# Latent values evicted into the places of dead keys and masks; query latents, near latents and the first latent weight split elsewhere

## The chip, the cores and the metric

The program runs on one core of one Trainium2 chip. The core has a matrix engine (TensorE, PE in the tables), three engines for elementwise work (VectorE or DVE, ScalarE or ACT, GpSimd or POOL), and queues that start transfers (SP's above all). The metric is the time of one execution in microseconds, as the median of several runs; less is better.

## The reference

Two transformer layers run over 128 context tokens and 512 latent tokens with the same weights. The first layer mixes tokens by two kinds of heads, eight of each: multi-head latent attention (MLA), whose keys and values are expanded from a short latent vector per token, and neighbourhood attention on a grid of width 64. The second has grouped-query attention. Each is followed by a SwiGLU block. All is float32. The change lies at the seam of the two kinds of heads in the first layer:

```python
def mla_expand(ckv, w_ukv, k_rope):
    kv = (ckv @ w_ukv).reshape(b, L, MLA_HEADS, MLA_NOPE_DIM + MLA_V_DIM)
    k_nope, v = kv[..., :MLA_NOPE_DIM], kv[..., MLA_NOPE_DIM:]
    k_r = jnp.broadcast_to(k_rope[:, :, None, :], (b, L, MLA_HEADS, MLA_ROPE_DIM))
    return jnp.concatenate([k_nope, k_r], axis=-1), v

def even_mixer_latent(h, c_ckv, c_krope, c_nk, c_nv, w_in, q_norm, w_uq, kv_norm, w_ukv, rpb, w_out, cos, sin):
    q, ckv, krope, nq, nk, nv = even_project(h, w_in, q_norm, w_uq, kv_norm, w_ukv)   # q = rms_norm(cq) @ w_uq
    q = jnp.concatenate([q[..., :MLA_NOPE_DIM], apply_rope(q[..., MLA_NOPE_DIM:], cos, sin)], axis=-1)
    krope = apply_rope(krope[:, :, None, :], cos, sin)[:, :, 0, :]
    k_lat, v_lat = mla_expand(ckv, w_ukv, krope)
    k_ctx, v_ctx = mla_expand(c_ckv, w_ukv, c_krope)
    a_mla = attend_blocked(q, jnp.concatenate([k_lat, k_ctx], axis=1),
                           jnp.concatenate([v_lat, v_ctx], axis=1), MLA_SCALE)
    a_na = neighbourhood_attention(nq, nk, nv, c_nk, c_nv, rpb)
    return jnp.concatenate([a_mla.reshape(b, L, -1), a_na.reshape(b, L, -1)], axis=-1) @ w_out

def reference(...):
    for l in range(DEPTH):                       # two layers; context (xp) and latents (xs) alike
        hs = modulate(rms_norm(xs, norm_mix[l]), sh1_s, sc1_s)
        out_s = even_mixer_latent(hs, ...) if l % 2 == 0 else odd_mixer_latent(hs, ...)
        xs = xs + g1_s * out_s
        hs = modulate(rms_norm(xs, norm_ffn[l]), sh2_s, sc2_s)
        xs = xs + g2_s * swiglu(hs, w_ffn_in[l], w_ffn_out[l])
    y_sample = rms_norm(xs, norm_final)
```

## The kernel before

Tokens stand in the columns, 640 of them (512 latents, then 128 of context), features in the 128 partitions. Every operand of a matrix product is kept as two tiles of a rounded format: a high part, which ScalarE writes by a copy, and a low part, the rest, which VectorE writes by a subtraction. This is called a split here. A product is three matmuls: high by high, high by low, low by high (`mm3`). The names end in `h` and `l` for the two parts.

Work is written as small pieces, and a string sets their order: `NA_FIRST`, `NA_ORDER` and `NA_LAST` for the eight neighbourhood heads (`for h in range(8)`), `MLA_FIRST`, `MLA_ORDER` and `MLA_LAST` for the eight MLA heads. `sequence` runs the pieces of a string one after the other. TensorE follows the strings; on ScalarE and VectorE a scheduler orders what the pieces issue, and `after(inst, fn)` keeps an instruction behind another one of the same engine. Each engine works strictly in its own order.

A neighbourhood head h has these pieces. `s0` and `s1` make the scores of four blocks of queries (`ns`), VectorE adds the mask and bias `bm` and takes the maximum (`np`, `nm`), ScalarE takes the exponentials, GpSimd divides by the sums. In the string of the next head stand its tail pieces: `t0` to `t2` transpose the weights (`nt`) and split them (`nts`, in `pt_split`), `v0` to `v2` multiply them with the values (`no`), and the result is added up in `oN`. `sp`, `pt` and `pv` (`npp`) are the same for the context tokens. Two tiles `bm` are used in turn, keys `nk0` and `nk1` are made for two heads at a time, and `nkc` holds the cached keys.

In the last two heads, h = 6 and 7, the work for MLA is woven in, since no projections are left there:

- `latents()` splits the latent vectors `ckv`: the `far` ones (`ck`, the 512 latents) and the `near` ones (`ckp`, cached and context). It runs behind h = 5, in front of the strings of h = 6.
- `mla_w(0)` splits the first MLA weight, `wm`.
- `x0` in h = 6 splits the query latents (`cqs`). `k0` and `k1` make the keys of the first two MLA heads (`mk`) and split them into `kT` and `kTp`; `mk` uses `far` latents first, `near` ones in `k1`.
- `x` in h = 7 splits the rotary keys `kr` into their places in `kT` and `kTp`.
- `u0` and `u1` make the first MLA query (`mq`); `b0` to `b3` multiply four blocks of latents with the value weight `wmv` (`mv_product`, banks `mv`), `b4` and `b5` follow within the first MLA head.
- The products `b0` to `b3` stay in their banks until the neighbourhood pool `ab` is closed. Then the tiles `mv` are opened in the next pool, `cp`, and `vsplit` evicts them.

The first MLA scores (`ms`, `mla_scores`) use the same banks, opened anew by `open_y(s=2)`.

Of the kernel before, what the change touches and what calls it, by code (L numbers as in the profile page):

```python
# [50 lines left out]
def body(ctx, tc, xT, vecs, crow, wm0, wm0g, wm1, wA, wNV, wNA, wMK, wMV, wOA, wGQ, wGK, wGV, wOC,  # L51
# [326 lines left out]
    def pt_split(ps, n, pool, name):  # L378
        bufs = 5 if pool.name == "cp" else 3
        h = pool.tile([P, 512], F32R, tag="pth", bufs=bufs, name=name + "h")  # L380
        l = pool.tile([P, 512], F32R, tag="ptl", bufs=bufs, name=name + "l")
        S.activation(h[:, :n], ps[:, :n], AF.Copy)
        V.tensor_tensor(l[:, :n], ps[:, :n], f(h[:, :n]), ALU.subtract)
# [60 lines left out]
    def vsplit(dst, src):  # L444

        s3 = src.rearrange("p (h d) -> p h d", d=64)
        S.activation(dst[:, :, 0:64], s3, AF.Copy)
        V.tensor_tensor(dst[:, :, 64:128], s3, f(dst[:, :, 0:64]), ALU.subtract)
# [62 lines left out]
    with tc.tile_pool(name="start", bufs=1) as big:  # L511
# [143 lines left out]
    nc.sync.dma_start(ckf, cnkT)  # L655
    nkc = ab.tile([P, 8, P], F32R, name="nkc")
    for r in range(2):
# [53 lines left out]
    def na_k(p):  # L711
        get = wna(p, 1)
        ks = [ab.tile([P, 1024], F32R, tag=f"nk{r}", bufs=1, name=f"nk{p}{r}") for r in range(2)]
        nqk[p][2] = ks
        out = []
        for c, (c0, c1) in enumerate(((0, 256), (256, T))):
            def done(ps, c=c):
                if c == 1:
                    kf = ab.tile([P, P], F32, tag="nkf", bufs=1, name=f"nkf{p}")
                    S.activation(kf, ps[:, 256:384], AF.Copy)  # L720
                    nc.gpsimd.dma_start(o_nkT[p], kf)
                for r in range(2):
# [6 lines left out]
                    mark[0] = S.activation(h, src, AF.Copy), V.tensor_tensor(l, src, f(h), ALU.subtract)
                    if c == 0:  # L730
                        G.tensor_scalar(ks[r][:, 768:896], f(ks[r][:, 0:P]), 1.0, 0.0, ALU.mult, ALU.add)
                        for i in (2, 4):
                            G.tensor_scalar(ks[r][:, P * i:P * i + P], f(nkc[:, 2 * p + r, :]), 1.0, 0.0, ALU.mult, ALU.add)
            out += pieces_of(f"nk{p}{c}", qbanks[c], get, hh, hl, list(range(KT)), c0, c1, done)
        return out

    bms = [ab.tile([P, 3, 384], F32, name=f"bm{i}") for i in range(2)]
    for bm in bms:
# [83 lines left out]
    def latents():  # L822
        cc = load(cckvT.rearrange("u p n -> p u n"), 256, "cc")
        near = [ring.tile([P, T], F32R, tag="x", name=f"ckp{c}") for c in "hl"]
        far = [[ring.tile([P, T], F32R, tag="h" + c, name=f"ck{c}{u}") for u in range(2)] for c in "hl"]
        for u in range(2):
            after(mark[0][0], lambda: S.activation(far[0][u][:, :NS], ckv[u][:, :NS], AF.Copy))
            after(mark[0][1], lambda: V.tensor_tensor(far[1][u][:, :NS], ckv[u][:, :NS], f(far[0][u][:, :NS]), ALU.subtract))
        nh, nl = [t[:, :512].rearrange("p (u n) -> p u n", u=2) for t in near]
        src = cc.rearrange("p (u n) -> p u n", u=2)  # L830
        after(mark[0][0], lambda: S.activation(nh[:, :, 0:P], src, AF.Copy))
        after(mark[0][1], lambda: V.tensor_tensor(nl[:, :, 0:P], src, f(nh[:, :, 0:P]), ALU.subtract))
        for u in range(2):
            after(mark[0][0], lambda: S.activation(nh[:, u, P:], ckv[u][:, NS:T], AF.Copy))
            after(mark[0][1], lambda: V.tensor_tensor(nl[:, u, P:], ckv[u][:, NS:T], f(nh[:, u, P:]), ALU.subtract))
        return far, [[t[:, 256 * u:256 * u + 256] for u in range(2)] for t in near]

# [55 lines left out]
    def mv_product(i, bk):  # L893
        def run():
            mvb.append(bk(f"mv{i}"))
            for u in range(2):
                a, b = [t[u][:, i % 4 * P:(i % 4 + 1) * P] for t in lat[i // 4]]
                mm3(mvb[i], a, b, wmv[0][:, 512 * u:512 * (u + 1)], wmv[1][:, 512 * u:512 * (u + 1)], u == 0, u == 1)
            if mv:
                vsplit(mv[i], mvb[i])  # L900
        return run

    mv = []

    def mq_ring(h):
# [5 lines left out]
                "s0 q0 t0 t1 q1 m0 q2 s1 v0 t2 sp q3 q4 v1 q5 q6 q7 m1 v2 m2")  # L911
    NA_LAST = "s0 t0 t1 s1 x0 v0 t2 pt k0 sp v1 k1 v2 pv", "s0 t0 t1 u0 s1 u1 v0 t2 b0 sp x v1 b1 v2"
    for h in range(8):
# [52 lines left out]
    nc.sync.dma_start(tq, tabM)  # L966
# [1255 lines left out]
```

## Time and profile before

| | |
|---|---|
| median of 3 runs | 1495.97 us (1495.92 to 1497.59) |
| profiled execution | 1495.85 us, of which the span of its instructions 1494.1 |
| mean granted TensorE clock in it | 0.993 |
| TensorE busy | 1445.6 us, 97% of the span |
| VectorE busy | 1210.5 us, 81% |
| ScalarE busy | 762.8 us, 51% |
| GpSimd busy | 207.3 us, 14% |
| read and written in memory | 192.23 and 34.69 MB, 152 GB/s |

The profile shows one execution. "Idle before" and brackets name what ended an engine's waiting. A row of the timeline has its start and length in us, the engine, the line, the operation, what it writes and reads, and how many there are. The granted clock is the share of TensorE's full clock in a stretch. Busy time on TensorE counts slow work too, so the clock has to be read beside it.

### The profile page before, as it was taken

The numbers are of one execution on the slowest core, as the hardware profiler recorded it, in microseconds if no ns is written. First come the engines' busy times: TensorE is split into PE (matmuls) and PEld (weight loads), VectorE is DVE, ScalarE is ACT, GpSimd is POOL, SyncE is SP. The second block draws the span as 40 slices with busy tenths as digits, with TensorE's granted clock in tenths as the row PEclk, the third lists the DMA queues.
The fourth block names the chain that finished last, engine by engine and source line by source line (L and its number), as shares of the span: only waits on it lengthen the run. The fifth ranks groups of instructions, "written<-read, shape, count | busy, mean of one in ns | idle before, by whom it ended". The sixth has DMA issues, their size and how long they took to land.

```text
span 1494.1 us, 25710 instructions
## 1 busy us (share of the span) xinstructions
PE 1445.6 (97%) x9785; PEld 1395.6 (93%) x9785; DVE 1210.5 (81%) x2278; ACT 762.8 (51%) x1509; POOL 207.3 (14%) x298
## 2 busy tenths in 40 slices
PE   5999988999999999999999999999999999999996
PEld 4988878889999999999999999989999999999996
DVE  5786687986899999977998878775899999954496
ACT  5445677873755454441123666663755555542242
POOL 0325634432000000000001312222000000000000
PEclk9999999999999999999999999999999999999998
DMA  9544410105155555569764311003155555668522
GB/s 373 215 146 155 150 58 18 43 29 191 50 180 173 187 180 180 181 214 337 272 214 132 114 33 37 33 20 130 49 180 178 181 193 206 211 222 309 194 85 71
DMA packets 79900, 228.59 MB, mean 153 GB/s; under 512 B 8865, under 2 KB 14273, under 8 KB 79393
## 3 DMA queue, kind: packets, MB, share of 16 engines
q1 hardware_dynamic: 76544, 219.40, 42.9%
q0 software_dynamic: 1600, 5.14, 0.9%
q10 hardware_dynamic: 1632, 2.43, 0.5%
q8 instruction: 76, 1.25, 0.3%
q14 instruction: 48, 0.39, 0.1%
HBM read 192.23 MB, written 34.69 MB: 152 GB/s over the span
## 4 chain that ended last, share of the span: by engine, by line
PE 84%; DVE 7%; ACT 5%; issue 2%; DMA 1%; DVEq 0%; ACTq 0%; SPq 0%
PE fg L63 20%; PE fd L63 9%; PE fo L63 8%; PE fu L63 6%; PE gq L63 3%; PE nk L63 2%; PE fo_0b L63 1%; PE fo_2b L63 1%; PE gs L63 1%; PE nq L63 1%; PE fo_2a L63 1%; PE fo_0a L63 1%; PE go L63 1%; PE mod L63 1%; PE ms L63 1%
## 5 line engine op out<-in xcount | busy, mean ns | idle before, releaser
L1759 DVE SCALAR_TENSOR_TENSOR junk<-wm,cb 128x1024 bf16<-128x1024 f32 x62 | 75.7, 1220 | 5.7 <-DMA wm<-in_wm 5.1
L1211 ACT ACTIVATE sg<-g 128x320 f32<-128x320 f32 x34 | 16.0, 472 | 114.9 <-DVE g L1211 114.9
L63 PE MATMUL gq<-h10h,wgq 128*128 128x320 f32 x256 | 66.7, 318 | 0.0
L255 POOL TENSOR_SCALAR h10h<-h10t,gs,mods 128x320 fp32r<-128x320 f32 x4 | 3.6, 891 | 429.5 <-DVE h10t L249 427.8
L1211 DVE SCALAR_TENSOR_TENSOR junk<-wm,cb 128x1024 bf16<-128x1024 f32 x50 | 61.0, 1221 | 0.8
L1211 DVE TENSOR_TENSOR wY<-s,wY 128x1024 fp32r<-128x1024 f32 x40 | 48.8, 1219 | 1.2 <-ACT wY L1211 1.1
L1211 DVE TENSOR_TENSOR wZ<-s,wZ 128x1024 fp32r<-128x1024 f32 x40 | 48.8, 1219 | 0.0
L63 PEld LDWEIGHTS gq<-h10h,wgq 128*128 128x128 f32 x256 | 45.0, 188 | 0.9 <-PE gtp L67 0.2
L1211 ACT ACTIVATE wZ<-s 128x1024 fp32r<-128x1024 f32 x40 | 42.4, 1060 | 0.1
L1211 ACT ACTIVATE wY<-s 128x1024 fp32r<-128x1024 f32 x40 | 42.0, 1049 | 0.0
L1941 ACT ACTIVATE gp<-gs,gb,rq 128x640 f32<-128x640 f32 (+1 forms) x40 | 31.8, 796 | 16.1 <-DVE gb L1940 15.8
L63 PE MATMUL gq<-h10l,wgq 128*128 128x320 f32 x128 | 39.5, 308 | 0.0
L63 PE MATMUL fg<-h11E,wW 128*128 128x320 f32 x240 | 38.7, 310 | 0.0
L63 PE MATMUL fg<-h01q,wX 128*128 128x320 f32 x240 | 38.6, 309 | 0.0
L63 PE MATMUL fg<-h11q,wX 128*128 128x320 f32 x240 | 38.6, 309 | 0.0
L63 PE MATMUL fg<-h11N,wZ 128*128 128x320 f32 x240 | 38.6, 309 | 0.0
L63 PE MATMUL fg<-h01N,wZ 128*128 128x320 f32 x240 | 38.6, 309 | 0.0
L63 PE MATMUL fu<-h11q,wX 128*128 128x320 f32 x240 | 38.6, 309 | 0.0
L63 PE MATMUL fu<-h01q,wX 128*128 128x320 f32 x240 | 38.6, 309 | 0.0
L63 PE MATMUL fg<-h01E,wW 128*128 128x320 f32 x240 | 38.6, 309 | 0.0
L63 PE MATMUL fg<-h11C,wY 128*128 128x320 f32 x240 | 38.5, 309 | 0.0
L63 PE MATMUL fd<-h11q,wZ 128*128 128x320 f32 x240 | 38.5, 309 | 0.0
(3224 smaller groups left out, 5250.6 us busy)
## 6 DMA issues: line engine op xcount, KB each, us to landing
wm<-in_wm SPq DMA_DIRECT2D x48, 512.0 KB, 3.7
mraw<-in_wm SPq DMA_DIRECT2D x8, 1024.0 KB, 15.3
mraw<-in_wm SPq DMA_DIRECT2D x16, 512.0 KB, 3.7
hr_T<-sp_T SPq DMA_DIRECT2D x21, 320.0 KB, 5.8
hr_B<-sp_B SPq DMA_DIRECT2D x18, 320.0 KB, 6.4
mrow<-in_wm0g POOLq DMA_DIRECT2D x8, 512.0 KB, 6.4
wm<-in_wm0g SPq DMA_DIRECT2D x8, 512.0 KB, 3.5
x<-in_xT SPq DMA_DIRECT2D x8, 320.0 KB, 5.3
```

What stands on the lines that cost most here:

```text
L63: cls.last = nc.tensor.matmul(*a, **k)
L255: G.tensor_scalar(h[:, c0:c1], t, self.gsl[:, k, 0:1], self.ml[:, self.sh + k, 0:1], ALU.mult, ALU.add)
L1211: self.last = after(self.last, lambda: op(*a, **k))
L1759: def step(kind, at, line=lambda op, *a, **k: op(*a, **k)):
L1941: S.activation(dst, src, AF.Exp, bias=nb, scale=rq[:, j:j + 1], accum_out=ll[:, j:j + 1])
```

## The change

The four evictions that waited for the pool's end now follow their products at once. Five of the six value tiles lie in a new pool `aa`, which outlives `ab`, at the places of tiles that are no longer used by then: `nkc`, `nk0`, `bm0`, `nk1`, `bm1` (`tag` names the place). The near latents leave `latents()` for `latents_near`, called in `x0`; `x0` stands before `s1` instead of behind it, and the splits in it stand behind the last transposes' split (`cut`) instead of the last exponential or maximum (`mark`). The rotary keys (`x`) go from h = 7 to the end of h = 6. The first MLA weight is split between the two halves of the last keys. A second place with the same idea in the second layer (`wgq`, `valued`) is also written.

```diff
 def pt_split(ps, n, pool, name):
-        S.activation(h[:, :n], ps[:, :n], AF.Copy)
-        V.tensor_tensor(l[:, :n], ps[:, :n], f(h[:, :n]), ALU.subtract)
+        cut[0] = (S.activation(h[:, :n], ps[:, :n], AF.Copy),
+                  V.tensor_tensor(l[:, :n], ps[:, :n], f(h[:, :n]), ALU.subtract))
...
     sb = ExitStack()
+    sa = ExitStack()
+    aa = sa.enter_context(tc.tile_pool(name="aa", bufs=1, reuse_waits="tile"))
     ab = sb.enter_context(tc.tile_pool(name="ab", bufs=1, reuse_waits="tile"))
-    nkc = ab.tile([P, 8, P], F32R, name="nkc")
+    nkc = aa.tile([P, 8, P], F32R, tag="nkc", name="nkc")
...
 def na_k(p):
-        ks = [ab.tile([P, 1024], F32R, tag=f"nk{r}", bufs=1, name=f"nk{p}{r}") for r in range(2)]
+        ks = [aa.tile([P, 1024], F32R, tag=f"nk{r}", bufs=1, name=f"nk{p}{r}") for r in range(2)]
...
                     mark[0] = S.activation(h, src, AF.Copy), V.tensor_tensor(l, src, f(h), ALU.subtract)
+                    if c == 0 and p == 3 and r == 1:
+                        mla_w(0, mark[0])
...
-    bms = [ab.tile([P, 3, 384], F32, name=f"bm{i}") for i in range(2)]
+    bms = [f(aa.tile([P, 3, 384], F32R, tag=f"bm{i}", name=f"bm{i}")) for i in range(2)]
...
 def latents():
+        return far, [[t[:, 256 * u:256 * u + 256] for u in range(2)] for t in near], near, cc
+
+    def latents_near(near, cc):
         nh, nl = [t[:, :512].rearrange("p (u n) -> p u n", u=2) for t in near]
-        after(mark[0][0], lambda: S.activation(nh[:, :, 0:P], src, AF.Copy))
+        after(cut[0][0], lambda: S.activation(nh[:, :, 0:P], src, AF.Copy))
...
 def mv_product(i, bk):
-            if mv:
-                vsplit(mv[i], mvb[i])
+            if i < 5:
+                mv[i] = aa.tile(([P, 9, P] if i in (2, 4) else [P, 8, P]), F32R, tag=("nkc", "nk0", "bm0", "nk1", "bm1")[i], name=f"mv{i}")
+            vsplit(mv[i], mvb[i])
...
-    NA_LAST = "s0 t0 t1 s1 x0 v0 t2 pt k0 sp v1 k1 v2 pv", "s0 t0 t1 u0 s1 u1 v0 t2 b0 sp x v1 b1 v2"
+    NA_LAST = "s0 t0 t1 x0 s1 v0 t2 pt k0 sp v1 k1 v2 x pv", "s0 t0 t1 u0 s1 u1 v0 t2 b0 sp v1 b1 v2"
...
-                    for t, q in zip(rsplit(cq[u], f"cqs{u}", mark[0]), qlat):
+                    for t, q in zip(rsplit(cq[u], f"cqs{u}", cut[0]), qlat):
                         q.append(t)
+                latents_near(*rest_lat)
...
         if h == 5:
-            lat = latents()
-            mla_w(0, mark[0])
+            *lat, near, cc = latents()
+            rest_lat = near, cc
...
-    mv += [cp.tile([P, 8, P], F32R, name=f"mv{i}") for i in range(6)]
-    for i in range(4):
-        vsplit(mv[i], mvb[i])
+    mv[5] = cp.tile([P, 8, P], F32R, name="mv5")
...
-        get = lazy(lambda: unit(wGQ[h], 1024, f"wgq{h}"))
+        get = lazy(lambda: unit(wGQ[h], 1024, f"wgq{h}", behind=valued[0] if h == 1 else None))
...
     for i in (0, 1, 2, 3, 5, 4):
-        S.activation(gvh[i], srcs[i], AF.Copy)
-        V.tensor_tensor(gvl[i], srcs[i], f(gvh[i]), ALU.subtract)
+        valued[:] = [(S.activation(gvh[i], srcs[i], AF.Copy), V.tensor_tensor(gvl[i], srcs[i], f(gvh[i]), ALU.subtract))]
```

TensorE's rows stand in the same order before and after. What moves stands on ScalarE and VectorE. On VectorE, ahead of the first maximum of h = 7 (the row `np_0` with `bm`), before, with the sums `oN` of the last tail and the value weight's split:

```order
L852 TENSOR_TENSOR kTp<-mk_2559,kTp 64x128 x2
L394 TENSOR_TENSOR oN_1990<-no_2513,nhs_2578 64x448
L394 TENSOR_TENSOR oN_1990<-no_2513,nhs_2578 64x64
L185 TENSOR_TENSOR wmv<-wmvr,wmv 128x1024
L440 TENSOR_TENSOR oN_1990<-npp2o,npp2h 64x128 x2
L771 ISA np_0_2606,nm_2591<-ns_00_2600,bm_1010 128x384
```

and the same place now:

```order
L861 TENSOR_TENSOR kTp<-mk_2562,kTp 64x128
L396 TENSOR_TENSOR oN_1993<-no_2516,nhs_2581 64x448
L396 TENSOR_TENSOR oN_1993<-no_2516,nhs_2581 64x64
L861 TENSOR_TENSOR kTl_2425<-kr,kTh_2423 64x512
L861 TENSOR_TENSOR kTl_2426<-kr,kTh_2424 64x512
L861 TENSOR_TENSOR kTl_2425<-kr,kTh_2423 64x128
L861 TENSOR_TENSOR kTl_2426<-kr,kTh_2424 64x128
L861 TENSOR_TENSOR kTp<-kr,kTp 64x128 x2
L442 TENSOR_TENSOR oN_1993<-npp2o,npp2h 64x128 x2
L185 TENSOR_TENSOR wmv<-wmvr,wmv 128x1024
L778 ISA np_0_2621,nm_2606<-ns_00_2615,bm_1013 128x384
```

The six rows that read the rotary keys `kr` have moved ahead of that maximum. On VectorE ahead of the second pair of maxima of h = 6, where the query latents `cqs` and the near latents `ckp` stand, before:

```order
L415 TENSOR_REDUCE npp3m_2546<-npp3s_2543 128x1
L375 RECIPROCAL nr_3r<-nl_2434 128x1
L454 TENSOR_TENSOR cqs0l<-cqr_587,cqs0h 128x640
L454 TENSOR_TENSOR cqs1l<-cqr_592,cqs1h 128x640
L832 TENSOR_TENSOR ckpl<-cc,ckph 128x2x128
L835 TENSOR_TENSOR ckpl<-ckvr_735,ckph 128x128
L835 TENSOR_TENSOR ckpl<-ckvr_740,ckph 128x128
```

and now:

```order
L375 RECIPROCAL nr_0r<-nl_2431 128x1
L457 TENSOR_TENSOR cqs0l<-cqr_590,cqs0h 128x640
L375 RECIPROCAL nr_1r<-nl_2431 128x1
L457 TENSOR_TENSOR cqs1l<-cqr_595,cqs1h 128x640
L842 TENSOR_TENSOR ckpl<-cc,ckph 128x2x128
L845 TENSOR_TENSOR ckpl<-ckvr_738,ckph 128x128
L845 TENSOR_TENSOR ckpl<-ckvr_743,ckph 128x128
L778 ISA np_2_2500,nm_2430<-ns_10_2494,bm_1012 128x384
```

The five split rows stood behind that pair of maxima (and behind the last sum's reciprocal, `nr_3r`) and now stand ahead of it. On VectorE ahead of the first maximum of MLA (`mn`), where the value products `mv` are evicted, before:

```order
L383 TENSOR_TENSOR npp3ptl<-npp3t,npp3pth 128x256
L394 TENSOR_TENSOR oN_2431<-no_2789,nhs_2809 64x448
L394 TENSOR_TENSOR oN_2431<-no_2789,nhs_2809 64x64
L440 TENSOR_TENSOR oN_2431<-npp3o,npp3h 64x128 x2
L448 TENSOR_TENSOR mv_2836<-mv_2698,mv_2836 128x8x64
L448 TENSOR_TENSOR mv_2837<-mv_2733,mv_2837 128x8x64
L448 TENSOR_TENSOR mv_2838<-mv_2775,mv_2838 128x8x64
L448 TENSOR_TENSOR mv_2839<-mv_2792,mv_2839 128x8x64
L448 TENSOR_TENSOR mv_2840<-mv_2858,mv_2840 128x8x64
L984 TENSOR_REDUCE mn_0_2874<-ms_0_2867 128x1
```

and now:

```order
L451 TENSOR_TENSOR mv_2791<-mv_2784,mv_2791 128x8x64
L383 TENSOR_TENSOR npp3ptl<-npp3t,npp3pth 128x256
L451 TENSOR_TENSOR mv_2811<-mv_2804,mv_2811 128x8x64
L396 TENSOR_TENSOR oN_2428<-no_2801,nhs_2824 64x448
L396 TENSOR_TENSOR oN_2428<-no_2801,nhs_2824 64x64
L442 TENSOR_TENSOR oN_2428<-npp3o,npp3h 64x128 x2
L451 TENSOR_TENSOR mv_2867<-mv_2860,mv_2867 128x8x64
L993 TENSOR_REDUCE mn_0_2877<-ms_0_2870 128x1
```

The fourth product's eviction (`mv_2811`) has gone ahead of the last tail's sums; only the fifth is left behind them.

More of the change, by code (lines that the diff above doesn't have):

```diff
@@ L381, in pt_split @@
         l = pool.tile([P, 512], F32R, tag="ptl", bufs=bufs, name=name + "l")
-        S.activation(h[:, :n], ps[:, :n], AF.Copy)
-        V.tensor_tensor(l[:, :n], ps[:, :n], f(h[:, :n]), ALU.subtract)
+        cut[0] = (S.activation(h[:, :n], ps[:, :n], AF.Copy),
+                  V.tensor_tensor(l[:, :n], ps[:, :n], f(h[:, :n]), ALU.subtract))
         return h, l
+    cut = [None]
     def tr(out, in_):
@@ L446, in vsplit @@
         s3 = src.rearrange("p (h d) -> p h d", d=64)
+        dst = dst[:, 0:8, :]
         S.activation(dst[:, :, 0:64], s3, AF.Copy)
@@ L828, in latents @@
             after(mark[0][1], lambda: V.tensor_tensor(far[1][u][:, :NS], ckv[u][:, :NS], f(far[0][u][:, :NS]), ALU.subtract))
+        return far, [[t[:, 256 * u:256 * u + 256] for u in range(2)] for t in near], near, cc
+    def latents_near(near, cc):
         nh, nl = [t[:, :512].rearrange("p (u n) -> p u n", u=2) for t in near]
         src = cc.rearrange("p (u n) -> p u n", u=2)
-        after(mark[0][0], lambda: S.activation(nh[:, :, 0:P], src, AF.Copy))
-        after(mark[0][1], lambda: V.tensor_tensor(nl[:, :, 0:P], src, f(nh[:, :, 0:P]), ALU.subtract))
+        after(cut[0][0], lambda: S.activation(nh[:, :, 0:P], src, AF.Copy))
+        after(cut[0][1], lambda: V.tensor_tensor(nl[:, :, 0:P], src, f(nh[:, :, 0:P]), ALU.subtract))
         for u in range(2):
-            after(mark[0][0], lambda: S.activation(nh[:, u, P:], ckv[u][:, NS:T], AF.Copy))
-            after(mark[0][1], lambda: V.tensor_tensor(nl[:, u, P:], ckv[u][:, NS:T], f(nh[:, u, P:]), ALU.subtract))
-        return far, [[t[:, 256 * u:256 * u + 256] for u in range(2)] for t in near]
+            after(cut[0][0], lambda: S.activation(nh[:, u, P:], ckv[u][:, NS:T], AF.Copy))
+            after(cut[0][1], lambda: V.tensor_tensor(nl[:, u, P:], ckv[u][:, NS:T], f(nh[:, u, P:]), ALU.subtract))
     KPART = ((0, 512), (512, 640), (640, 768))
@@ L898, in run @@
                 mm3(mvb[i], a, b, wmv[0][:, 512 * u:512 * (u + 1)], wmv[1][:, 512 * u:512 * (u + 1)], u == 0, u == 1)
-            if mv:
-                vsplit(mv[i], mvb[i])
+            if i < 5:
+                mv[i] = aa.tile(([P, 9, P] if i in (2, 4) else [P, 8, P]), F32R, tag=("nkc", "nk0", "bm0", "nk1", "bm1")[i], name=f"mv{i}")
+            vsplit(mv[i], mvb[i])
         return run
-    mv = []
+    mv = {}
     def mq_ring(h):
@@ L936, in query_latents @@
                 for u in range(2):
-                    for t, q in zip(rsplit(cq[u], f"cqs{u}", mark[0]), qlat):
+                    for t, q in zip(rsplit(cq[u], f"cqs{u}", cut[0]), qlat):
                         q.append(t)
+                latents_near(*rest_lat)
             pieces["x0"] = query_latents
+            pieces["x"] = lambda: k_set((slice(64, 128), slice(0, 64)), (0, 1, 2), [kr[:, a:b] for a, b in KPART])
             pieces.update(named("k", k_pieces(0, ybank)))
@@ L942, in body @@
             wmv = unit(wMV, 1024, "wmv", behind=mark[0])
-            pieces["x"] = lambda: k_set((slice(64, 128), slice(0, 64)), (0, 1, 2), [kr[:, a:b] for a, b in KPART])
             pieces.update(named("u", mq_ring(0)))
@@ L1078, in body @@
     sb.close()
+    sa.close()
     l0.close()
@@ L1879, in keys @@
                 kps[v, c] = kns[v][:, c0:c1]
-    gqs, rope0 = {}, []
+    gqs, rope0, valued = {}, [], []
     def gqa_q(h):
-        get = lazy(lambda: unit(wGQ[h], 1024, f"wgq{h}"))
+        get = lazy(lambda: unit(wGQ[h], 1024, f"wgq{h}", behind=valued[0] if h == 1 else None))
         qh = gp.tile([P, T], F32R, tag="gqh", bufs=2, name=f"gqh{h}")
```

## The prediction

> **What bounds the kernel now.** I read the page first: busy shares and the chain that ended last.
>
> ```profile
> span 1494.1 us, 25710 instructions
> PE 1445.6 (97%) x9785; PEld 1395.6 (93%) x9785; DVE 1210.5 (81%) x2278; ACT 762.8 (51%) x1509; POOL 207.3 (14%) x298
> PE 84%; DVE 7%; ACT 5%; issue 2%; DMA 1%; DVEq 0%; ACTq 0%; SPq 0%
> ```
>
> TensorE (PE) carries 84% of the chain; time is won where PE waits or runs slowly. The edits that move rows all sit between the sixth head of the neighbourhood attention and the first MLA head, about 187 to 240 us (heads are counted from 1 here; h in the code is one less). PE's waits from 180 to 260 us, longest in total first:
>
> ```profile
> PE ms L63 <- DVE mv L448: 3.4, 1, 3.4
> PE mk L63 <- DVE ckpl L835: 2.8, 1, 2.8
> PE no L63 <- ACT nts_0h L382: 1.6, 1, 1.6
> PE no L63 <- DVE nts_0l L383: 1.0, 1, 1.0
> PE npp3t L67 <- DVE oN L394: 0.8, 1, 0.8
> ```
>
> Next I cut that place into windows of 3.4 us (columns: stretch, length, PE busy and count, granted clock, DMA):
>
> ```profile
> 198.80:202.20 3.40, 1.61 (x12) 1.00 0.01 2
> 202.20:205.60 3.40, 2.38 (x11) 0.50 0.36 116
> 205.60:209.00 3.40, 3.40 (x16) 0.50 0.01 2
> 226.10:229.50 3.40, 0.53 (x3) 1.00 0.59 193
> 229.50:232.90 3.40, 2.91 (x9) 0.50 0.00 0
> ```
>
> After a window with PE busy 1.61 or 0.53 of 3.40 us the granted clock is 0.50. It came back after windows with 3.40 and 2.91 busy, not after 2.38. So each long wait is paid twice: at half clock, work takes about double (eight transposes below: 207.44 to 209.00, against 192.03 to 192.82). The first drop costs half of 2.38 + 3.40, 2.9 us; the second half of 2.91, 1.5 us. PE in order of time (start, length, row, wait in brackets):
>
> ```profile
> 192.03 1.03 PE L67 MATMUL nt<-ident,np 128*128 128x128 f32 x8
> 192.82 0.42 PE L63 MATMUL ns<-nk,nqh 128*128 128x384 f32 x1
> 203.22 0.58 PE L63 MATMUL mk<-ckpl,wm 128*128 128x256 f32 x1 [2.81 <-DVE ckpl L835]
> 207.44 1.82 PE L67 MATMUL nt<-ident,np 128*128 128x128 f32 x8
> 209.00 0.41 PE L63 MATMUL mq<-cqs0h,wm 128*128 128x320 f32 x1
> 210.80 0.44 PE L63 MATMUL ns<-nk,nqh 128*128 128x384 f32 x1 [0.31 <-DVE nm L771]
> 221.02 0.41 PE L67 MATMUL npp3t<-ident,npp3p 128*128 128x128 f32 x2 [0.84 <-DVE oN L394]
> 225.03 0.68 PE L63 MATMUL mv<-wmv,ckph 128*128 128x512 f32 x2
> 229.99 0.87 PE L63 MATMUL ms<-kTh,mqh 128*128 128x320 f32 x2 [3.36 <-DVE mv L448]
> ```
>
> And VectorE (DVE), the engine that PE waits for here, with one GpSimd row of the same time:
>
> ```profile
> 195.12 0.94 DVE L185 TENSOR_TENSOR wm<-wm0r,wm 128x768 fp32r<-128x768 f32 x1
> 195.99 0.20 DVE L774 TENSOR_SCALAR nn<-nm 128x1 f32<-128x1 f32 x2
> 197.63 0.16 DVE L375 RECIPROCAL nr_1r<-nl 128x1 f32<-128x1 f32 x1 [0.18 <-ACT np L775]
> 200.38 0.17 DVE L375 RECIPROCAL nr_3r<-nl 128x1 f32<-128x1 f32 x1 [0.31 <-ACT np L775]
> 200.94 0.95 DVE L454 TENSOR_TENSOR cqs0l<-cqr,cqs0h 128x640 fp32r<-128x640 f32 x1 [0.39 <-ACT cqs0h L453]
> 203.29 1.38 DVE L852 TENSOR_TENSOR kTl<-mk,kTh 64x512 fp32r<-64x512 f32 x2
> 205.84 0.59 DVE L852 TENSOR_TENSOR kTl<-mk,kTh 64x128 fp32r<-64x128 f32 x2 [0.98 <-ACT kTp L849]
> 209.57 0.58 DVE L440 TENSOR_TENSOR oN<-npp2o,npp2h 64x128 f32<-64x128 f32 x2 [0.49 <-ACT npp2h L438]
> 210.18 0.56 DVE L771 CUSTOM_DVE_ANT_0 np<-ns,bm 128x384 f32<-128x384 f32 x1
> 215.80 0.69 DVE L852 TENSOR_TENSOR kTl<-kr,kTh 64x512 fp32r<-64x512 f32 x1
> 216.61 2.13 DVE L852 TENSOR_TENSOR kTl<-kr,kTh 64x512 fp32r<-64x512 f32 x3
> 216.92 1.29 POOL L881 TENSOR_TENSOR mql<-mqt,mqh 128x320 fp32r<-128x320 f32 x1
> 218.75 0.59 DVE L852 TENSOR_TENSOR kTp<-kr,kTp 64x128 fp32r<-64x128 f32 x2
> 227.36 3.08 DVE L448 TENSOR_TENSOR mv<-mv,mv 128x512 fp32r<-128x512 f32 x5
> ```
>
> From 193 to 210 us DVE is idle only for the bracketed 2.35 us. It bounds that stretch, and it is where the change adds work.
>
> **The change part by part.** The order of the matmuls is the same in both programs, so only waits and the clock can move.
>
> *Latent values evicted at once.* Before, the first MLA score at 229.99 stands behind five evictions in one group (227.36, 3.08 us), because its two banks held the third and fourth product. Now those two are evicted as soon as they are made, ahead of the last tail rows. PE finishes the fourth product some 1.4 us before 225.03 (tail rows of head 8 stand between) and needs its bank after the fifth product, which takes 229.99 - 3.36 - 225.03 = 1.6 us; a ScalarE (ACT) eviction and a DVE one take about 0.6 each in that group, so there are about 1.5 us in hand. The wait goes: 3.36 us, and with it the half clock, 1.5 us. What is late next is the table tq for the second head, needed some 4 us after that score; a transfer queued (225.22 below) behind the same row as before, so it keeps its distance to the work. The evictions fall where DVE has room only if it isn't behind; see the third rival.
>
> *Near and query latents, and the rotary keys.* The split of the near latents moves behind the first transposes of head 7 and the query latents into the same place, both ahead of the second pair of score maxima. The 2.81 wait of mk mostly goes; what is late next is its bank, which waits for the maxima that stand behind five split rows. DVE gets to them from 195.1 (the weight split there is gone) by 1.5 for small rows and the transposes' splits, about 2.4 for the five (0.95 for the first, shorter ones after) and 1.0 for two maxima: 200.0. I take mk at 199.8. But the rotary key splits (six DVE rows on kr) move from the end of head 8 to the end of head 7, ahead of the first maximum of head 8 (row 210.18), which PE needs for its next score bank, the row at 210.80. That is the added wait. Behind it on PE is everything of head 8.
>
> When does DVE get there? 210.18, less the weight split (195.12 to 195.99, 0.87), plus the rotary rows, less the idle time that can be filled. The rotary rows took 0.69 + 2.13 + 0.59 = 3.4 in the trace; the same shapes from mk took 1.38 + 0.59 and, with the last pair, 0.59 more, 2.56 in all. I take 2.56, since the slow group ran beside a long GpSimd row (216.92), and that row comes later in head 8 than the new place, and keep 3.4 as the bound. Of the 2.35 idle I let 1.85 be filled and 0.5 stay. So 210.18 - 0.87 + 2.56 - 1.85 = 210.0: PE passes its score bank 0.2 us earlier than before (bounds: 1.0 earlier when rows pack tighter, 0.9 later with 3.4).
>
> When does PE get there? From 203.22 to 210.80 it took 7.58 us, of which 0.31 waiting and 2.9 lost to the half clock, so 4.4 at full clock. From 199.8, with about 1.3 of small waits on the same DVE, that is 205.5, and PE then stands still for about 5 us. All that the removed waits (mk, and the 1.6 + 1.0 on nts) bring is used up there.
>
> A stop of 5 us covers more than half of some window, so the clock drops. Where the window edges fall isn't to be chosen: with the first edge 1.8 us or more into the stop the clock drops there and is back two windows later; at 1.0 to 1.8 it drops one edge later; under 1.0 the third window holds too little work to bring it back, as 2.38 did above. PE then works 2.7 to 6 us at half clock and loses half of it: 1.3 to 3.0, I take 2.2. The Trainium skill (TensorE: Matmul & The Clock Gate, Part 1: The HAM clock gate) says that the window is free-running, 3413 ns; the drops at 202.2 and 229.5, eight windows apart, agree.
>
> The wait of 0.84 at 221.02 goes too: DVE rows ahead of it (rotary keys) have left, and PE comes 2 us later.
>
> *Weight split at head 6.* Transfers of the near latents, the first weight and the table tq on SP's queue, and the DVE row behind the last keys:
>
> ```profile
> 168.45 0.38 SPq L164 DMA_DIRECT2D cc<-in_cckvT  x1
> 175.47 0.34 SPq L164 DMA_DIRECT2D wm0r<-in_wMK  x1
> 225.22 0.33 SPq L966 DMA_DIRECT2D tq<-in_tabM  x1
> 190.97 0.55 DVE L729 TENSOR_TENSOR nk<-nk,nk 64x384 fp32r<-64x384 f32 x1 [2.47 <-ACT nk L729]
> ```
>
> The first MLA weight's split (0.94) goes into those 2.47 us, in which DVE waits for ACT and ACT for PE's last keys: nothing on the path, and if the row slipped past 190.97 it would cost its 0.9 there. The weight's and the near latents' transfers change places on SP's queue, with a bias table between them. Issued at 168 and 175 and used past 188, both have over 10 us in hand, which hides the change of order; were that gone, PE would wait for a landing. *Places.* Evictions now wait for the last readers of keys and masks, which are done by then; cost 0. *GpSimd* does one low query half one row later; no wait of PE above names it: 0. *The edge on the second grouped-query weight* moves no row: 0.
>
> **Sum**, against the profiled execution (1495.85, span 1494.1 and 1.75 around it, 0.12 under the median): 0.2 + 0.84 - 2.2 + 3.36 + 1.5 = 3.7 us gained. From there to the end PE runs almost without waits, so it stays: 1492.3 at the level of the median.
>
> **Rivals.** (1) The clock doesn't drop at the new wait, or the wait is short since DVE rows pack tighter: 2.2 more, up to 1.0 more, about 1489.7. Against it: a wait of 2.81 sufficed before. The same page (HAM oscillation) holds idle gaps up to about 3.4 us harmless; by that a wait 1.6 us shorter than mine would keep the clock, but the trace's 2.81 with the drop at 202.2 disagrees.
>
> (2) DVE is later: 3.4 for the rotary rows (0.9 more) and the dear clock case (0.8 more) leave 2.0: 1494.0. For it: the only rows on kr that the trace has are the slow ones.
>
> (3) The change doesn't do what it says: the fourth value product isn't evicted in time, because DVE, late through head 8, comes to it more than 1.5 us later than I think, and 229.99's wait stays. Then 0.2 + 0.84 - 2.2 is all: 1497.1.
>
> (4) Slower: the clock stays at half through all of head 8, whose many short transposes keep windows thin. From 210.6 to the score there are 229.99 - 3.36 - 0.84 - 210.80 = 15.0 us of work; doubled, 15 lost instead of 2.2: 1505.1. It turns into a loss from 5.9 us lost, 11.8 us at half clock, the fourth window. Against it: the same kind of rows brought it back at 209.0 after one full window.
>
> **Chances.** Forecast (gain 2.5 to 5) 0.50, (1) 0.13, (2) 0.24, (3) 0.08, (4) 0.05. What a measurement tells from no change is 0.2%, 3.0 us, so faster means under 1493.0: nine tenths of the forecast and (1), 0.59. Same: the rest of the forecast, (2) and most of (3), 0.33. Slower 0.08. The range runs from (1) with everything in its favour, 1489.2, to short of (3), 1495.9; the forecast's own is 1491 to 1493.5.
>
> **What would show it.** Right: no wait of ms on mv, PE waiting 4 to 6 us for nm at head 8's second bank, the granted clock 0.50 right behind that, and no 0.50 at the first MLA score. Wrong if that wait is under 2 us or over 7, or if a new wait over 1 us stands in the first MLA head.

## The result, and the profile after

The changed kernel takes 1493.07 us in the median (1491.25 to 1495.14), the kernel before 1496.90 (1495.01 to 1497.84) in the same comparison; the ratio is 0.9977, 95% interval 0.9969 to 0.9985. That is 3.4 us faster (2.2 to 4.6). The prediction was 1492.3 within 1489.2 to 1495.9, and faster. Its profiled execution took 1493.43. Of its 13 runs the four with a mean granted clock of 0.990 or 0.991, the profiled one among them, took 1493.4 to 1495.1 us, the other nine 1491.3 to 1493.7. First the page of the changed kernel: span, busy time of the engines, chain that ended last.

```profile
span 1491.6 us, 25707 instructions
PE 1445.5 (97%) x9785; PEld 1395.5 (94%) x9785; DVE 1210.0 (81%) x2278; ACT 763.3 (51%) x1509; POOL 207.8 (14%) x298
PE 85%; DVE 7%; ACT 4%; DMA 2%; issue 2%; DVEq 0%; SPq 0%; ACTq 0%
```

The busy times are those of before within 0.5 us, so what moved is waiting and the clock. TensorE's longest waits from 180 to 260 us:

```profile
PE ns L63 <- DVE nm L778: 4.7, 1, 4.7
PE ns L63 <- DVE kTl L861: 1.6, 1, 1.6
PE no L63 <- DVE nn L781: 1.5, 1, 1.5
```

The waits of `ms` on `mv`, `mk` on `ckpl` and `npp3t` on `oN` are gone; the first row is the new wait at head 8's second score bank (the buffer that TensorE writes scores to; it is free again when the maxima have read it), at 213.35 in the list in order of time:

```profile
192.53 0.44 PE L63 MATMUL ns<-nk,nqh 128*128 128x384 f32 x1 [0.50 <-DVE nk L734]
196.86 0.50 PE L63 MATMUL no<-nts_0l,nv 128*128 128x512 f32 x1 [1.50 <-DVE nn L781]
201.73 0.28 PE L63 MATMUL mk<-ckph,wm 128*128 128x256 f32 x1
205.48 0.42 PE L63 MATMUL ns<-nk,nqh 128*128 128x384 f32 x1 [1.61 <-DVE kTl L861]
213.35 0.69 PE L63 MATMUL ns<-nk,nqh 128*128 128x384 f32 x1 [4.65 <-DVE nm L778]
224.77 0.38 PE L67 MATMUL npp3t<-ident,npp3p 128*128 128x128 f32 x2
229.82 0.45 PE L63 MATMUL ms<-kTh,mqh 128*128 128x320 f32 x2
232.95 0.31 PE L63 MATMUL mq<-cqs0h,wm 128*128 128x320 f32 x1
```

The granted clock (the column behind PE's busy time and count), in windows laid on the edges of its drops:

```profile
194.55:197.96 3.41, 1.75 (x10) 1.00 0.00 0
197.96:201.37 3.41, 3.41 (x13) 0.50 0.17 46
208.20:211.61 3.41, 0.50 (x4) 1.00 0.01 2
211.61:215.03 3.42, 1.68 (x6) 0.50 0.31 89
215.03:218.44 3.41, 3.41 (x13) 0.50 0.20 38
225.27:228.68 3.41, 3.41 (x24) 1.00 0.00 0
228.68:232.09 3.41, 3.41 (x19) 1.00 0.58 192
```

Half clock for two windows right behind the new wait, none at the first MLA score, as forecast; and one that was not forecast, at 197.96, behind a wait of only 1.50.

Executions differ by when the windows begin, so two spans compare badly. I compare one stretch, from the score row that waits 0.50 for `nk` (192.53) to the first `mq` row behind the first MLA score (232.95): 40.42 us. In the kernel before it runs between these rows, 42.98 us:

```profile
191.57 0.44 PE L63 MATMUL ns<-nk,nqh 128*128 128x384 f32 x1 [0.50 <-DVE nk L729]
...
234.55 0.31 PE L63 MATMUL mq<-cqs0h,wm 128*128 128x320 f32 x1
```

So this pair of executions shows 2.56 us gained in the stretch. From there to the end the waits are the same in both within 0.3 us. The lengths of that rest are not: over all the kernels below it took 1258.4 to 1261.8 us, so gains in the runs and in the stretch can differ by some us.

### The profile page after: what moved, and what is told of

It reads as the page before. It is cut to its first block, busy times and chain, and to the rows that moved or that the text cites. A ratio compares the mean times of both kernels' runs of the same rounds, so it can differ in the third digit from the quotient of the medians.

```text
span 1491.6 us, 25707 instructions
## 1 busy us (share of the span) xinstructions
PE 1445.5 (97%) x9785; PEld 1395.5 (94%) x9785; DVE 1210.0 (81%) x2278; ACT 763.3 (51%) x1509; POOL 207.8 (14%) x298
## 4 chain that ended last, share of the span: by engine, by line
PE 85%; DVE 7%; ACT 4%; DMA 2%; issue 2%; DVEq 0%; SPq 0%; ACTq 0%
PE fg L63 21%; PE fd L63 9%; PE fo L63 8%; PE fu L63 6%; PE gq L63 3%; PE nk L63 2%; PE nq L63 1%; PE fo_2b L63 1%; PE fo_0b L63 1%; PE gs L63 1%; PE fo_2a L63 1%; PE fo_0a L63 1%; PE go L63 1%; PE mod L63 1%; DMA mraw<-in_wm 1%
## 5 line engine op out<-in xcount | busy, mean ns | idle before, releaser
L63 PE MATMUL fg<-h11E,wW 128*128 128x320 f32 x240 | 38.7, 310 | 0.0
L63 PE MATMUL fg<-h01C,wY 128*128 128x320 f32 x240 | 38.5, 309 | 0.0
```

Source lines behind the costliest of these rows:

```text
L63: cls.last = nc.tensor.matmul(*a, **k)
```

## Experiments

Each was timed in five rounds against the kernel before (the whole change in the 13 runs above). They ran on two chips, so kernels are compared by their ratio to the kernel before on the same chip. "Gain" is one minus the ratio, times the median of before in that comparison, with its 95% interval; "stretch" is the length defined above in the one profiled execution, and in brackets what it is shorter than before's 42.98.

| kernel | ratio (interval) | gain, us | stretch, us |
|---|---|---|---|
| whole change | 0.9977 (0.9969 to 0.9985) | 3.4 (2.2 to 4.6) | 40.42 (2.56) |
| eviction alone | 0.9955 (0.9943 to 0.9968) | 6.7 (4.8 to 8.5) | 37.67 (5.31) |
| all but eviction | 1.0009 (1.0000 to 1.0018) | -1.3 (-2.7 to 0.0) | 44.07 (-1.09) |
| rotary keys back | 0.9966 (0.9953 to 0.9978) | 5.1 (3.3 to 7.0) | 37.15 (5.83) |
| latents back | 0.9969 (0.9959 to 0.9979) | 4.6 (3.1 to 6.1) | 37.98 (5.00) |
| rotary lows on GpSimd | 0.9953 (0.9940 to 0.9965) | 7.0 (5.2 to 9.0) | 37.76 (5.22) |
| eviction, query lows on GpSimd | 0.9986 (0.9977 to 0.9995) | 2.1 (0.7 to 3.4) | 41.32 (1.66) |
| rotary back, far and query lows on GpSimd | 0.9939 (0.9925 to 0.9952) | 9.1 (7.2 to 11.2) | 35.20 (7.78) |
| eviction, weight split early | 0.9969 (0.9956 to 0.9981) | 4.6 (2.8 to 6.6) | 36.73 (6.25) |
| exponentials first | 0.9979 (0.9970 to 0.9988) | 3.1 (1.8 to 4.5) | 38.44 (4.54) |
| the fastest, copies late | 0.9963 (0.9951 to 0.9976) | 5.5 (3.6 to 7.3) | 37.82 (5.16) |
| the same, one query low on DVE | 0.9966 (0.9954 to 0.9977) | 5.1 (3.4 to 6.9) | 38.19 (4.79) |
| weight split back | 0.9987 (0.9978 to 0.9996) | 1.9 (0.6 to 3.3) | 41.24 (1.74) |

My theory (1): the gain is the wait at the first MLA score with its half clock, and the rest of the change gives part of it back at head 8's second score bank. Rival (2): the gain comes from the earlier latents at `mk`. The edge on the weight in the second layer stays in all these kernels and is not tested by itself; in the traces the split of `wgq1` stands 38.7 us behind that of `wgq0` before and after, and the wait of `gs` on `gvl` is 2.2 in both.

**The eviction alone.** The kernel before, with this part of the change (and that edge):

```diff
+            if i < 5:
+                mv[i] = aa.tile(..., tag=("nkc", "nk0", "bm0", "nk1", "bm1")[i], name=f"mv{i}")
+            vsplit(mv[i], mvb[i])
```

> The kernel before with one part of the change: the value products are evicted as soon as they are made, into the places of dead keys and masks. Latents, rotary keys and first weight split stand as before. Theory 1 (the gain is the wait at the first MLA score and the half clock behind it; the rest of the change earns nothing): the wait of 3.36 goes and the 1.5 lost at half clock with it, the mk wait of about 2.8 stays, no new wait for nm over 1 us: 4.9 us under the kernel before, 4.0 to 5.5. That would be faster than the whole change. Theory 2 (the gain comes from the earlier latents at mk): within 1 us of the kernel before.

Its waits from 186 to 240 us and the first MLA score:

```profile
PE mk L63 <- DVE ckpl L840: 1.8, 1, 1.8
PE no L63 <- ACT nts_0h L382: 1.6, 1, 1.6
PE no L63 <- DVE nts_0l L383: 1.0, 1, 1.0
PE ns L63 <- DVE nm L776: 0.7, 1, 0.7
...
226.88 0.45 PE L63 MATMUL ms<-kTh,mqh 128*128 128x320 f32 x2
```

No wait and no half clock at the score, the waits of `no` on `nts` as before, and a gain of 6.7: twice that of the whole change, and the intervals do not overlap. The forecast of 4.9 lies within the interval. Theory 2 falls.

**All but the eviction.**

```diff
-            vsplit(mv[i], mvb[i])
+            if mv:
+                vsplit(mv[i], mvb[i])
...
+    mv += [cp.tile([P, 8, P], F32R, name=f"mv{i}") for i in range(6)]
+    for i in range(4):
+        vsplit(mv[i], mvb[i])
```

> The whole change but for the eviction: the third and fourth value product wait in their banks for the end of the neighbourhood heads, as before. Theory 1: no gain, since what mk and the transposes no longer wait is stood out again at the second score bank of head 8, with a half clock behind it: 0 to 1.5 us slower than the kernel before, the wait of the first MLA score on mv back at 2.5 to 3.5. Theory 2: 3 to 4 us faster than the kernel before, as the whole change is.

```profile
PE ns L63 <- DVE nm L778: 3.7, 1, 3.7
PE ms L63 <- DVE mv L451: 3.4, 1, 3.4
```

Both waits stand side by side, and there is no gain. Against the whole change (1.0009 less 0.9977) the eviction is worth 4.8 us there (3.0 to 6.6 from the two intervals); the forecast's 3.36 + 1.5 lies in it. The two profiled executions differ by 3.65 in the stretch; in this one no half clock stands behind the wait of 3.36.

**Rotary keys back in head 8.**

```diff
-    NA_LAST = "... k0 sp v1 k1 v2 x pv", "... b0 sp v1 b1 v2"
+    NA_LAST = "... k0 sp v1 k1 v2 pv", "... b0 sp x v1 b1 v2"
```

> The whole change, but the rotary keys are split in head 8 again, behind its first score rows, as before. Theory 1 (the six DVE rows on kr, 2.57 us, and the three ACT copies in front of the exponentials, 0.95, make most of the wait of 4.65 for nm at the second score bank of head 8): that wait falls to 1 to 2 us, the first maximum of head 8 comes 2.5 to 3.5 us earlier, and the whole is 2 to 3.5 us faster than with the whole change, about 1490.3. Theory 3 (the wait comes from rows stretched beside GpSimd and from late exponentials): it stays over 3.5 us, time within 0.5 us of the whole change. Theory 4 (the rows only move the wait to the end of head 8): the wait for nm falls, but a wait of 1 us or more stands at the first MLA score, time within 1 us of the whole change.

PE's row at the bank, and VectorE's first maximum of head 8:

```profile
210.03 0.69 PE L63 MATMUL ns<-nk,nqh 128*128 128x384 f32 x1 [0.57 <-DVE nm L778]
...
209.41 0.56 DVE L778 CUSTOM_DVE_ANT_0 np<-ns,bm 128x384 f32<-128x384 f32 x1
```

From the stretch's start the maximum comes after 209.41 - 192.76 = 16.65 us, against 212.74 - 192.53 = 20.21 with the whole change: 3.6 earlier, and the wait shrinks from 4.65 to 0.57 (PE, at half clock from 206.2, comes 0.5 later). The new strings moved less than expected. On ACT three copies of `kr` stand as early in the stretch as with the whole change, two of them (201.32, 0.95) right ahead of the exponential at 202.29, and VectorE still waits for that:

```profile
203.10 0.16 DVE L375 RECIPROCAL nr_2r<-nl 128x1 f32<-128x1 f32 x1 [1.06 <-ACT np L782]
```

So it is the early place of the rotary rows on VectorE that made the wait (theory 3 falls), and no wait on `kTl` or `mv` stands at the first MLA score (theory 4 falls). The times do not show it by themselves: the intervals of this kernel and the whole change overlap.

**Latents back.** Query and near latents at their old places (`x0` behind `s1`, the near ones in `latents()`).

```diff
-    NA_LAST = "s0 t0 t1 x0 s1 v0 t2 ...
+    NA_LAST = "s0 t0 t1 s1 x0 v0 t2 ...
-                latents_near(*rest_lat)
```

> The whole change, but query and near latents are split at their old places, behind the second score maxima of head 7; rotary keys stay early. Theory 1 (what is saved at mk is swallowed by the later wait on the same DVE): the mk wait is back at 2 to 3 us with a half clock, the wait for nm at head 8 is shorter by as much, time within 0.8 us of the whole change. Theory 2 (the earlier latents earn the gain): 2 to 3.5 us slower than the whole change.

```profile
202.18 0.39 PE L63 MATMUL mk<-ckpl,wm 128*128 128x256 f32 x1 [2.58 <-DVE ckpl L842]
...
210.74 0.44 PE L63 MATMUL ns<-nk,nqh 128*128 128x384 f32 x1 [3.97 <-DVE nm L778]
```

The `mk` wait is back at 2.58, and it is no slower than the whole change (intervals overlap): theory 2 falls again. Theory 1 had the sizes wrong, too: the wait for `nm` is shorter by 0.7 and not by 2 to 3, and the half clock of `mk` did not come in this execution.

**Which half of the rotary keys.** Their low parts on GpSimd, ACT's copies left where they were:

```diff
-            V.tensor_tensor(l, src, h, ALU.subtract)
+            eng.tensor_tensor(l, src, h, ALU.subtract)      # eng is G for kr, V otherwise
```

> The whole change, with the six low parts of the rotary keys computed on GpSimd instead of DVE, at the same place in the program; ACT's copies of them stay. It tells the two halves of theory 1 apart. DVE half (the six rows, 2.57 us, stand ahead of the first maximum of head 8): the wait of 4.65 for nm falls to 1.5 to 2.5 us, time 1.5 to 3 us under the whole change, about 1490.5. ACT half (the copies make the exponentials late, and DVE only waits for these): the wait stays over 3.5 us, time within 0.7 us of the whole change. Either way GpSimd has to be done before the first MLA score; a wait of ms for kTl would show that it isn't.

```profile
208.61 0.69 PE L63 MATMUL ns<-nk,nqh 128*128 128x384 f32 x1 [2.15 <-DVE nm L778]
```

The wait falls by 2.50, and the gain is twice the whole change's, with intervals that do not overlap. From the stretch's start the maximum comes after 17.07 us, 3.14 earlier: 2.57 is what the six rows took on VectorE, and the rest goes with `mk`, which ran at full clock here (the reciprocal `nr_2r`, which waited 1.14 with the whole change, comes 0.66 earlier). PE came 0.6 earlier, too. No wait on `kTl` stands at the first MLA score. Together with the rotary keys back in head 8, this shows the rows on VectorE as the cause of most of the wait. The other half, ACT's order, I tried by itself:

```diff
-            pieces["x"] = lambda: k_set(...)
+            pieces["x"] = lambda: after(mark[0][0], lambda: k_set(...))
```

> The whole change, but ACT's copies of the rotary keys are issued behind the last exponential of head 7 (in the whole change three of them, 1.6 us, stand ahead of its last two exponentials). DVE keeps the six rotary rows ahead of the first maximum of head 8. If late exponentials make DVE idle 1.14 us there: that idle piece falls under 0.5, the wait for nm falls from 4.65 to 3.5 to 4.2, time 0.5 to 1.5 us under the whole change. If the six rows alone make the wait: it stays at 4.3 or more, time within 0.5 us of the whole change.

The idle piece of 1.14 is gone, and the first maximum of head 8 comes 18.83 us into the stretch instead of 20.21. But the wait is 4.65 as before and the time the same as the whole change's (0.9979 against 0.9977): PE came earlier by as much, its clock not having dropped at `mk` in that execution. The late exponentials are real in the trace; that they cost time is not shown.

**Weight split back**, behind `latents()` as before the change:

```diff
-                    if c == 0 and p == 3 and r == 1:
-                        mla_w(0, mark[0])
...
+            mla_w(0, mark[0])          # behind latents(), at h == 5
```

> The whole change, but the first latent weight is split where it was, behind the second pair of maxima of head 7's start. The prediction's step (the row moves into idle time and takes 0.87 us out of the path of DVE to the first maximum of head 8): with it back the wait for nm grows by 0.5 to 0.9 and the time by 0.5 to 1.5 us over the whole change. Rival (the row is worth nothing, since DVE waits there for exponentials and for GpSimd): wait and time within 0.4 us and 0.6 us.

The stretch grows by 0.82 and the gain falls by 1.5 (intervals overlap). That fits the forecast of 0.87 for this step, but does not show it: the first maximum comes 1.35 later in the stretch, but PE comes 2.5 later (half clock behind drops at 197.2 and 207.4), and so the wait went down, to 3.54, instead of up. The reverse, the early split added to the eviction alone, isn't clear:

```diff
+                    if c == 0 and p == 3 and r == 1:
+                        mla_w(0, mark[0])
...
-            mla_w(0, mark[0])
```

> The eviction part alone (1489.5) with the first latent weight split behind the last neighbourhood keys, as the whole change has it. Prediction's reading (the row goes into idle time of DVE and ACT, and 0.9 us of DVE leave the stretch ahead of the transposes' split): the waits on nts and mk shrink by 0.5 to 1.5 in all, time 0 to 1.5 us under the eviction part alone. Rival (a row beside GpSimd's key copies is stretched and holds the keys up): up to 1 us over it, with a longer wait for nk.

The two waits on `nts` shrink, from 1.59 and 0.99 to 0.87 and 0.80, but that of `mk` grows from 1.75 to 2.59, so in all nothing is saved there. The stretch is 0.94 shorter than with the eviction alone, the gain 2 us less, with intervals that overlap. What the early split is worth stays open.

**GpSimd in place of VectorE.** Four tries at something faster. The eviction alone, with the low parts of the query latents on GpSimd:

```diff
-        after(at[1], lambda: V.tensor_tensor(l, src, f(h), ALU.subtract))
+        after(at[1], lambda: eng.tensor_tensor(l, src, f(h), ALU.subtract))      # G for cqs
```

> The eviction part alone (1489.5), with the two low parts of the query latents (1.6 us of DVE ahead of the near latents at mk) on GpSimd. If DVE's row order is what holds mk: its wait of 1.8 falls under 0.5, the half clock at 205 goes or comes once fewer, 1 to 2.5 us under the eviction part alone, about 1487.7. Rival: DVE rows beside GpSimd rows take as much longer as was saved, time within 0.6 us of the eviction part alone.

The wait of `mk` did not fall, it doubled, and 4.6 of the 6.7 are lost. PE, VectorE and GpSimd there:

```profile
206.74 0.58 PE L63 MATMUL mk<-ckpl,wm 128*128 128x256 f32 x1 [3.69 <-DVE ckpl L840]
...
204.74 1.74 DVE L837 TENSOR_TENSOR ckpl<-cc,ckph 128x256 fp32r<-128x256 f32 x1 [2.21 <-POOL cqs0l L457]
...
203.17 1.53 POOL L457 TENSOR_TENSOR cqs0l<-cqr,cqs0h 128x640 fp32r<-128x640 f32 x1
204.66 1.54 POOL L457 TENSOR_TENSOR cqs1l<-cqr,cqs1h 128x640 fp32r<-128x640 f32 x1
```

The near latents go into the place of the raw query latents (both have the tag `x` of one ring), so their row waits for `cqs0l`, which now stands behind GpSimd's normalisations; and then it runs beside `cqs1l` and takes 1.74 instead of 0.41. Neither of my two theories had that wait.

The whole change with the rotary keys back and the low parts of query and far latents on GpSimd; it starts on the far ones at 194.19, in time it stood idle:

```diff
-            after(mark[0][1], lambda: V.tensor_tensor(far[1][u][:, :NS], ...
+            after(mark[0][1], lambda: G.tensor_tensor(far[1][u][:, :NS], ...
```

> The whole change with the rotary keys back in head 8 (1490.7), and the low parts of the far and of the query latents (1.3 and 1.6 us of DVE) on GpSimd. If DVE's row order is what holds the first transposes' split and the second score bank: the waits of 1.5 and 1.9 fall to under 0.5 and under 1.2, no half clock between 195 and 215, 2 to 4 us under the version with the rotary keys back, about 1487.7. Rival: GpSimd comes late with the far latents and mk waits for them instead, time within 1 us.

```profile
196.09 0.50 PE L63 MATMUL no<-nts_0l,nv 128*128 128x512 f32 x1 [0.30 <-DVE nn L781]
...
194.19 2.54 POOL L835 TENSOR_TENSOR ckl<-ckvr,ckh 128x512 fp32r<-128x512 f32 x2 [1.35 <-ACT ckh L834]
```

1487.70 us, the lowest median of all: the wait of 1.50 is 0.30, and one half clock window is left, at 202.0 (none was forecast). It is faster than the version with the rotary keys back; from the eviction alone the intervals do not tell it apart. Two tries to better it, the rotary copies behind the last exponential of head 8, and one low part of the query latents back on VectorE:

```diff
-            pieces["x"] = lambda: k_set(...)
+            pieces["x"] = lambda: after(mark[0][0], lambda: k_set(...))
```

> The fastest version so far (low parts of far and query latents on GpSimd, rotary keys in head 8; 1487.7), with the rotary copies issued behind the last exponential of head 8, so that they leave the ACT rows ahead of the first maximum of head 8 (DVE waited 0.95 there for an ACT row). If ACT's order holds that maximum: the wait for nm falls from 1.8 to about 0.8, time 0.5 to 2 us under 1487.7. Rival: the six rotary rows, now 2.6 us of DVE late in head 8, hold up the value products' evictions, a wait of 0.5 or more at the transposes or the first MLA score, time within 1 us of 1487.7 or over it.

```diff
-                    for t, q in zip(rsplit(cq[u], f"cqs{u}", cut[0], G), qlat):
+                    for t, q in zip(rsplit(cq[u], f"cqs{u}", cut[0], (V, G)[u]), qlat):
                         q.append(t)
-                latents_near(*rest_lat)
+                    if u == 0:
+                        latents_near(*rest_lat)
```

> As the run before, but of the query latents only the second low part is on GpSimd, and the near latents are split between the two. DVE rows with two operands took as long as the GpSimd row beside them where both ran at once (1.74 and 1.84 against 0.41 and 0.48). If these collisions hold the mk keys: its wait of 1.1 goes under 0.4, and no or one half clock window is left between 195 and 215; time 0 to 2 us under the run before. Rival: DVE, with 0.8 us more of its own, is late at the second pair of maxima of head 7, mk waits for nm, time 0 to 1.5 us over it.

```profile
219.56 0.41 PE L67 MATMUL npp3t<-ident,npp3p 128*128 128x128 f32 x2 [1.70 <-DVE oN L396]
...
215.05 2.50 DVE L861 TENSOR_TENSOR kTl<-kr,kTh 64x512 fp32r<-64x512 f32 x4
```

The rival of the first came true (rows of the first try): the rotary rows, 2.50 and 0.59, now stand ahead of `oN`, and the transposes wait 1.70, with a half clock window. The wait for `nm`, which was to fall to 0.8, is 1.71 (1.77 in the run that it starts from). The second has the same wait at the transposes, `mk` still waits 0.93, and it is no different from the first (5.1 against 5.5); what the split alone does can't be told from it.

## Why the prediction was right, and where its working was not

**Eviction: right.** 3.36 + 1.5 forecast; 3.36 + 1.43 in the traces (from the first MLA score to the `mq` row 4.56 before, 3.13 after), 4.8 in the runs of the whole change with and without it, 6.7 by itself. The fourth product was evicted in time, and `tq` did not become late.

**PE at the second bank: wrong.** The step is "Of the 2.35 idle I let 1.85 be filled and 0.5 stay". VectorE's busy time from the stretch's start to the first maximum of head 8, before and after (before's rows: 191.57, 210.18):

```profile
191.57:210.18 18.61, 15.99 (x45) 0.82 0.15 44
```

```profile
192.53:212.74 20.21, 17.92 (x50) 0.89 0.12 39
```

Idle went from 2.62 (the bracketed 2.35 and pieces too short for a bracket) to 2.29, so 0.33 was filled, not 1.85. The other two terms were good: the rotary rows took 1.98 + 0.59 = 2.57 (forecast 2.56, bound 3.4), the weight split left (0.87). The rest of 17.92 - 15.99 = 1.93, 0.23, is the net of other rows; those of the near latents took 0.72 and 0.79 beside GpSimd's, against 0.41 and 0.48 before. So the maximum came 1.6 later in the stretch instead of 0.2 earlier. Old idle pieces did close, but new ones opened. ACT and VectorE in order of time:

```profile
200.55 1.20 ACT L858 ACTIVATE kTh<-mk 64x512 fp32r<-64x512 f32 x2 [0.70 <-PE mk L63]
201.76 0.95 ACT L858 ACTIVATE kTh<-kr 64x512 fp32r<-64x512 f32 x2
202.74 0.62 ACT L782 ACTIVATE np<-np,nn 128x384 f32<-128x384 f32 x1
```

```profile
203.55 0.16 DVE L375 RECIPROCAL nr_2r<-nl 128x1 f32<-128x1 f32 x1 [1.14 <-ACT np L782]
208.48 1.98 DVE L861 TENSOR_TENSOR kTl<-kr,kTh 64x512 fp32r<-64x512 f32 x4
210.48 0.59 DVE L861 TENSOR_TENSOR kTp<-kr,kTp 64x128 fp32r<-64x128 f32 x2
212.74 0.55 DVE L778 CUSTOM_DVE_ANT_0 np<-ns,bm 128x384 f32<-128x384 f32 x1
```

The exponential at 202.74 stands behind copies of `mk` and `kr` on ACT, and the copy of `mk` waited 0.70 for PE, which ran at half clock. The other executions tell the two apart. The reciprocal `nr_2r`, 11.02 us into the stretch here, comes after 10.36 and 10.34 where `mk` ran at full clock and the copies stood as early (rotary lows on GpSimd, rotary keys back), and after 9.83 with the exponentials first. So about 0.7 of its lateness goes with the half clock and 0.5 with the copies of `kr`. The prediction had costed the moved rows on VectorE, but neither the copies that go with them on ACT nor a drop of the clock at `mk`.

**The new wait: right in size, not in place.** 4.65 against "about 5". Both ends are late: PE was there at 213.35 - 4.65 = 208.70, not 205.5, since it waited 1.50 and 1.61 on the way and made `mk` at half clock. Of the 1.6 + 1.0 on `nts`, which the prediction counted as removed, 0.16 and that 1.50 stayed. That two late ends left the size right is luck.

**The clock: right.** Two windows at half clock behind the wait. From the bank to `npp3t` the same work took 11.42 us (213.35 to 224.77) against 10.22 - 0.84 before: 2.04 lost, forecast 2.2. **The wait of 0.84** went, with the small gap behind it: from `npp3t` to the end of the fifth product 5.05 us against 5.61.

**The sum.** -1.6 + 0.84 + 0.56 - 2.04 + 3.36 + 1.43 = 2.55 in the profiled pair, forecast 3.7, and 3.4 in the runs. The forecast number is better than its working, and in part by luck: one term was 1.8 too good, 0.56 was missing, and the runs gain 0.8 more than the pair. The likely reason for the last is the drop at 197.96, which the wait of 1.50 brings in some executions only: with the same 1.50 it did not come in those with the rotary keys back, with their low parts on GpSimd, and with the exponentials first. This is argued from other kernels' executions, not shown on this one. **Rivals:** (1) fell with the drop at the new wait; that the rotary rows cost 3.4 (2) is refuted by 2.57, but its outcome, a later VectorE, came all the same, for the reasons above; that the fourth product is late (3) and that the half clock stays (4) did not happen. Two slips change little: nine tenths of 0.50 and 0.13 make 0.58, not 0.59, and of the "up to 1.0 more" in rival (1) the forecast already held 0.2.

## What to carry to other kernels

Split a change into its parts and time each: here one part was worth 6.7 us, and another, that filled an engine which paced the next stage, gave half of it back. When rows move to an earlier place, count them on every engine they run on, and let idle time in front of a pacing engine count as filled only if what ends each idle piece gets earlier too (here the late exponential). Before moving a row to an idle engine, ask whose memory place it frees, and which queue it will stand in.

## What was not expected of the hardware

**The clock followed how busy a window was, not how long a wait was.** I laid windows on the edges of the drops in all fourteen executions, from 186 to 240 us. Of 21 drops 20 came behind windows in which PE was busy 0.41 to 1.76 of 3.41 us, one behind 2.19 (at 202.0, the fastest kernel); full clock was kept after windows of 1.69 and 1.78, and after all others of 1.82 and more. A wait of 1.50 was enough at 197.96. And the same wait of 3.36 at the first MLA score that cost half clock in the kernel before cost none with all but the eviction, where a window's edge fell in its middle:

```profile
227.41:230.82 3.41, 1.78 (x10) 1.00 0.61 192
230.82:234.24 3.42, 1.69 (x10) 1.00 0.00 0
234.24:237.65 3.41, 3.41 (x23) 1.00 0.00 0
```

So about half a window, 1.7 us, divides all but one of them (ends of matmuls are modelled, so the limit is not sharp), and where the edges fall differs from one execution to the next. The Trainium skill (TensorE: Matmul & The Clock Gate, HAM oscillation) gives idle gaps of more than about 3.4 us as the limit; here a wait of 1.50 was enough, and one of 3.36 was not.

**VectorE and GpSimd rows held each other up.** `ckpl` (0.41 alone) took 1.74 from 204.74, up to 206.48, and GpSimd's `cqs1l` beside it ran from 204.66 to 206.20: VectorE's row ended 0.28 behind GpSimd's. The other way round, in the whole change GpSimd's row at 197.65 took 1.78 beside the splits on VectorE, where the same shape took 0.59 at 203.81. The Trainium skill (SBUF — State Buffer, SBUF: two separate sides) says that a VectorE operation with two inputs in SBUF, the memory on the chip, and a GpSimd operation that reads SBUF exclude each other for the whole instruction; these rows agree.
